# State-space groups as a pipeline, with u and the outputs regrouped through DRAM

## The chip, the cores and the metric

The kernel runs on one core of a Trainium2 chip. The time is device microseconds of one launch. It is written with a tile framework: a scheduler fixes the order of the instructions on each engine when the kernel is built, and each engine then runs its own list in that order. TensorE does the matmuls, VectorE and ScalarE the elementwise work, GpSimd (called POOL in the profile) and SP mostly issue DMAs.

## What is computed

A decoder trunk of two layers over x of 512 positions and 1024 channels, all float32. In each layer one projection of the normalised x gives ten groups of 512 columns, four mixers work on them, and a second projection takes their gated results back to x:

```
for layer in range(DEPTH):                       # DEPTH = 2
    h = rms_norm(x, norm_g[layer])
    a_u, a_g, qd, kd, vd, b_g, c_x, c_g, m_q, m_g = split(h @ w_in[layer], 10)
    y_a = s5_mixer(a_u, ...)        # state space, below
    y_b = differential attention;  y_c = conv + RG-LRU;  y_m = attention to 256 memory tokens
    mixed = concat([y_a*silu(a_g), y_b*silu(b_g), y_c*silu(c_g), y_m*silu(m_g)])
    x = x + mixed @ w_out[layer]
return rms_norm(x, final_norm_g)
```

The state-space mixer has 32 groups of 16 channels, each with 64 complex states. With abar the diagonal of a group and bb its scaled input matrix:

```
x[t] = abar * x[t-1] + bb @ u[t]                 # complex, 64 states a group
y[t] = Re(C x[t]) + d * u[t]
ga, gb = split(gelu(y) @ w_glu);  y_a = ga * sigmoid(gb)
```

## The kernel before

**Projections.** Weights come in pieces of 512 KB (`raw`, two buffers). ScalarE rounds a piece to `whi` (L166), VectorE makes the rest `wlo` (L172), three buffers each, and a projection is three products: hi by hi, lo by hi, hi by lo, with 512 columns moving. In `cm_block` (matmuls L512) the weights are stationary and the result has channels on partitions; in `tm_block` (L532) h is stationary and the result has positions on partitions. The projection of u (`au`) uses `tm_block` with a strided view of h, `h_au`, that takes every fourth position, because the state space works on chunks of T = 4 positions, NC = 128 chunks.

**State space.** `s5` (L920 to L1057) is a generator. Each `yield` hands the turn back to the projections, and a number n in it asks for n ticks; a tick is twelve projection matmuls. First TensorE turns au to U (channel and step on partitions, chunk in the free dimension, 16 blocks), 32 transposes at L927. Then four groups f of four blocks follow one after the other, in each:

- the weights of the chunk's inputs on VectorE, turned by TensorE at L952 (the w-turn) and copied to WT; a small matmul with them (`ms`, L959) plus the direct term gives kq (VectorE), and eight DMAs from GpSimd's queue (L970) spread kq over MT, the matrix of the outputs inside a chunk;
- the states at chunk ends (L990, into `sc`), turned by the phase tables tcq and tsq to xr, scanned over the chunks at L1019 (eight scans), and turned back to xp, the state before each chunk;
- VV, the output weights of the states (VectorE);
- the outputs: U as stationary operand by MT (L1034), xp by VV (L1036), copied to yg at L1038.

After the last group 32 transposes (L1048) bring yg back to channels on partitions, the GELU follows (L1050), and yhi and ylo for the glu projection (matmuls L1215). `mpT`, `qm`, `bg` and others in the rows belong to the other mixers, which run beside it in the same way.

**Norm scale and end.** For layer 0 the norm's scale is broadcast to all 128 partitions by one DMA from ScalarE's queue (L246, `gnb`, 512 KB), and h is x times 1/rms times the scale in one VectorE instruction per half (L295). At the end each of four blocks of x is normalised and leaves in two stores of 256 KB, both from SP's queue (L1296 and L1297).

Of the kernel before, what the change touches and what calls it, by code (L numbers as in the profile page):

```python
# [17 lines left out]
P = 128  # L18
# [36 lines left out]
D_S5 = (1, 1, 1, 2, 2)  # L55
# [35 lines left out]
def tile_kernel(ctx: ExitStack, tc: tile.TileContext, A, out):  # L91
# [7 lines left out]
    sm2 = ctx.enter_context(tc.tile_pool(name="sm2", bufs=9))  # L99
# [96 lines left out]
    gnb = b4([P, D], "gnb")  # L196
# [20 lines left out]
    for l in range(DEPTH):  # L217
        for n in ORDER[l]:
# [14 lines left out]
            elif n in ("q", "k", "v", "au"):  # L233
# [166 lines left out]
    f2_re = const.tile([P, 32], F32, tag="f2_re", name="f2_re")  # L400
    f2_im = const.tile([P, 32], F32, tag="f2_im", name="f2_im")
# [89 lines left out]
    VV = [const.tile([P, 4, 2, T, 16], F32, tag=f"VV{i}", name=f"VV{i}") for i in range(2)]  # L491
    MT = const.tile([P, 2, T, 4, 16], F32, tag="MT", name="MT")
# [69 lines left out]

    def h_au():
        hi = [a.rearrange("p k (c s) -> p k s c", s=T) for a in cur["hi"]]
        lo = [a.rearrange("p k (c s) -> p k s c", s=T) for a in cur["lo"]]
        return ((lambda k, t: hi[k // 4][:, k % 4, t, :]), (lambda k, t: lo[k // 4][:, k % 4, t, :]))
# [279 lines left out]

    bbx = const.tile([P, 32, 16], F32, tag="bbx", name="bbx")
# [8 lines left out]
    def s5_params(l, R):  # L856
        while "par" in st.live:
            yield
        B, Cw = R["B"], R["Cw"]

# [54 lines left out]
    def au_evac(au):  # L915
        def f(s, a):
            S.copy(au[:, :, :, T - 1 - s, :].rearrange("p q g h -> p (q g) h"), a.rearrange("p (a h) -> p a h", h=16))
        return f

    def s5(l, R):  # L920
        au = R["au"]
# [8 lines left out]
        yg = b8([P, T, 16, 2, 16], "yg")  # L930
# [3 lines left out]
        for f in range(4):  # L934
            qs = slice(4 * f, 4 * f + 4)
# [12 lines left out]
            wd = t1.rearrange("p (q g) d h -> p q (g d h)", g=2)  # L948
# [380 lines left out]
```

## Time and profile before

| | |
|---|---|
| median of three runs | 917.92 us (917.91 to 918.27) |
| the profiled execution | 918.38 us, span 916.6 us |
| TensorE busy | 888.9 us, 97% |
| VectorE busy | 658.6 us, 72% |
| ScalarE busy | 510.6 us, 56% |
| GpSimd busy | 43.0 us, 5% |
| DMA | 90.59 MB, 99 GB/s mean |
| granted clock of TensorE | 0.999 of full speed |

The span is the profiled stretch of one execution; 1.8 us of the measured time lie outside it. A busy share is a mean over stages that differ: the span begins with 8.5 us without a matmul, and in the state-space rounds (215 to 338 us in layer 0, 650 to 800 us in layer 1) VectorE is far busier than its mean. A row of the profile names the line of the kernel, the engine and the operation, then what it writes and reads by the program's names without numbers (`xr<-u,u`). Bracketed text behind a row of a timeline is the time the engine sat idle before it and what ended that; a row without it followed at once.

### The profile page before, as it was taken

The numbers are of one execution on the slowest core, as the hardware profiler recorded it, in microseconds if no ns is written. First come the engines' busy times: TensorE is split into PE (matmuls) and PEld (weight loads), VectorE is DVE, ScalarE is ACT, GpSimd is POOL, SyncE is SP. The second block draws the span as 40 slices with busy tenths as digits, with TensorE's granted clock in tenths as the row PEclk, the third lists the DMA queues.
The fourth block names the chain that finished last, engine by engine and source line by source line (L and its number), as shares of the span: only waits on it lengthen the run. The fifth ranks groups of instructions, "written<-read, shape, count | busy, mean of one in ns | idle before, by whom it ended". The sixth has DMA issues, their size and how long they took to land.

```text
span 916.6 us, 12496 instructions
## 1 busy us (share of the span) xinstructions
PE 888.9 (97%) x4538; PEld 747.8 (82%) x4538; DVE 658.6 (72%) x1314; ACT 510.6 (56%) x1031; POOL 43.0 (5%) x94
## 2 busy tenths in 40 slices
PE   5999999999999999999999999999999999999997
PEld 4788888987888788888888888898878888788885
DVE  5984888678999946883374677764889988667343
ACT  6684787985433355821554578766645453854133
POOL 1001000001110100000100000000101110000000
PEclk9999999999999999999999999999999999999999
DMA  6733432212132226433343332432121313152322
GB/s 200 203 114 103 140 92 69 64 53 73 50 93 73 73 93 185 142 107 108 115 149 93 92 92 69 139 92 69 50 70 50 96 31 98 60 184 93 103 81 93
DMA packets 81072, 90.59 MB, mean 99 GB/s; under 512 B 23793, under 2 KB 58226, under 8 KB 81010
## 3 DMA queue, kind: packets, MB, share of 16 engines
q1 hardware_dynamic: 77986, 85.98, 30.1%
q10 hardware_dynamic: 720, 2.62, 0.8%
q0 software_dynamic: 2304, 1.18, 0.6%
q8 instruction: 36, 0.59, 0.3%
q14 instruction: 26, 0.21, 0.1%
HBM read 84.92 MB, written 4.19 MB: 97 GB/s over the span
## 4 chain that ended last, share of the span: by engine, by line
PE 69%; DVE 22%; ACT 6%; issue 2%; DMA 1%; DVEq 0%; SPq 0%; ACTq 0%
PE acc L532 38%; PE acc L512 12%; DVE u L340 5%; PE acc L1215 5%; DVE wlo L172 3%; DVE xr L1019 2%; PE tp L1036 2%; PE ms L677 1%; PE tp L305 1%; PE tp L830 1%; DVE VV L340 1%; PE sc L642 1%; DVE wt L340 1%; PE sc L643 1%; ACT whi L166 1%
## 5 line engine op out<-in xcount | busy, mean ns | idle before, releaser
L166 ACT CAST whi<-raw 128x1024 fp32r<-128x1024 f32 x136 | 143.2, 1053 | 227.9 <-PE acc L532 117.6
L172 DVE TENSOR_TENSOR wlo<-raw,whi 128x1024 fp32r<-128x1024 f32 x136 | 166.2, 1222 | 121.5 <-ACT whi L166 117.8
L512 PE MATMUL acc<-hThi,whi 128*128 128x512 f32 x384 | 153.8, 400 | 0.0
L512 PE MATMUL acc<-hThi,wlo 128*128 128x512 f32 x384 | 152.1, 396 | 0.0
L512 PE MATMUL acc<-hTlo,whi 128*128 128x512 f32 x384 | 152.0, 396 | 0.0
L532 PE MATMUL acc<-whi,hThi 128*128 128x512 f32 x256 | 104.1, 407 | 0.8 <-ACT whi L166 0.8
L532 PE MATMUL acc<-wlo,hThi 128*128 128x512 f32 x256 | 101.4, 396 | 0.0
L532 PE MATMUL acc<-whi,hTlo 128*128 128x512 f32 x256 | 101.0, 395 | 0.0
L532 PE MATMUL acc<-wlo,mxh 128*128 128x512 f32 x256 | 100.1, 391 | 0.0
L532 PE MATMUL acc<-whi,mxh 128*128 128x512 f32 x256 | 100.1, 391 | 0.0
L532 PE MATMUL acc<-whi,mxl 128*128 128x512 f32 x256 | 100.1, 391 | 0.0
L512 PEld LDWEIGHTS acc<-hThi,wlo 128*128 128x128 f32 x384 | 72.2, 188 | 14.5
L512 PEld LDWEIGHTS acc<-hThi,whi 128*128 128x128 f32 x384 | 72.3, 188 | 13.2
L512 PEld LDWEIGHTS acc<-hTlo,whi 128*128 128x128 f32 x384 | 72.4, 188 | 13.1
L532 PEld LDWEIGHTS acc<-whi,hThi 128*128 128x128 f32 x256 | 56.2, 220 | 9.0 <-ACT whi L166 1.2
L532 PEld LDWEIGHTS acc<-whi,hTlo 128*128 128x128 f32 x256 | 56.3, 220 | 7.8 <-DVE hTlo L308 0.2
L532 PEld LDWEIGHTS acc<-wlo,hThi 128*128 128x128 f32 x256 | 56.6, 221 | 7.2
L532 PEld LDWEIGHTS acc<-whi,mxl 128*128 128x128 f32 x256 | 48.1, 188 | 9.8
L532 PEld LDWEIGHTS acc<-wlo,mxh 128*128 128x128 f32 x256 | 48.1, 188 | 9.7
L532 PEld LDWEIGHTS acc<-whi,mxh 128*128 128x128 f32 x256 | 48.1, 188 | 9.7
L970 POOL DMA_DIRECT2D MT<-kq x64 | 32.1, 509 | 364.2 <-DVE kq L340 363.9
L653 ACT ACTIVATE e<-sc,nmx 128x128 f32<-128x128 f32 (+3 forms) x64 | 33.1, 524 | 6.6 <-DVE nmx L649 5.4
(310 smaller groups left out, 1643.8 us busy)
## 6 DMA issues: line engine op xcount, KB each, us to landing
raw<-in_w_in_dram SPq DMA_DIRECT2D x80, 512.0 KB, 3.7
raw<-in_w_out_dram SPq DMA_DIRECT2D x32, 512.0 KB, 3.3
raw<-in_w_mem_kv_dram SPq DMA_DIRECT2D x16, 512.0 KB, 3.4
x<-in_x_dram SPq DMA_DIRECT2D x8, 512.0 KB, 5.2
raw<-in_s_w_glu_dram SPq DMA_DIRECT2D x16, 256.0 KB, 2.9
mt<-in_mem_dram SPq DMA_DIRECT2D x4, 512.0 KB
xd<-x SPq DMA_DIRECT2D x4, 512.0 KB, 4.2
x<-xd SPq DMA_DIRECT2D x4, 512.0 KB, 5.5
```

What stands on the lines that cost most here:

```text
L166: S.copy(hi, wbuf[j])
L172: V.tensor_tensor(out=lo, in0=raw, in1=hi, op=ALU.subtract)
L305: lastins["pe"] = PE.transpose(pt[:, k, :], h[:, kk * 128:(kk + 1) * 128], ident)
L340: V.tensor_tensor(out=o, in0=a, in1=b, op=op)
L512: PE.matmul(a[j][:, :ncol], w[:, kk, c], h(k), start=(hf == 0 and i == 0), stop=(hf == 1 and i == 3 * nh - 1))
L532: PE.matmul(a[t], h(k, t), w[:, kk, :], start=(p == 0 and kk == 0 and i == 0), stop=(p == np_ - 1 and kk == 1 and i == 2))
L642: PE.matmul(s[:, m, :M], qh[:, m, h, :], kT[m][:, h, :M], start=True, stop=False)
L653: S.activation(e[:, m, :N], s[:, m, :N], AF.Exp, bias=nmx[:, m:m + 1], scale=0.125, accum_out=sm[:, m:m + 1])
L970: G.dma_start(out=MT[g * 64 + 64 - n:g * 64 + 64, g, t], in_=kq[g * 64:g * 64 + n])
L1019: V.tensor_tensor_scan(out=xr_[i][:, j, :], data0=dec, data1=xr_[i][:, j, :], initial=0.0, op0=ALU.mult, op1=ALU.add)
L1036: PE.matmul(y[:, j, :], xp[i][:, j, :], VV[i][:, j].rearrange("p g t h -> p (g t h)"), start=False, stop=(i == 1))
L1215: PE.matmul(a, w[:, k, s, j * 128:(j + 1) * 128], h[:, 2 * hf + k, :], start=(hf == 0 and i == 0), stop=(hf == 1 and i == 5))
```

## The change

- **Start.** Only one row of the norm's scale is loaded (4 KB), and TensorE spreads it over the partitions by two matmuls with a row of ones, into PSUM (`sc`); h reads it from there in layer 0.
- **au.** It is made by `cm_block`, weights stationary, h moving, so channels are on partitions. Each of its four blocks is stored to DRAM (`aud`) by GpSimd's queue, and eight DMAs of 128 KB read it back as U. The 32 transposes of L927 are gone.
- **Outputs.** MT and VV are now the stationary operands and U and xp the moving ones (both were laid out anew for it, so MT's eight DMAs move pieces of 64 bytes instead of 256). The result has outputs on partitions and chunks in the free dimension. It is copied to `ys`, stored to DRAM (`yd`) by four DMAs and read back as `yl` by one, all in GpSimd's queue. The GELU reads yl. The 32 transposes of L1048 are gone.
- **Pipeline.** The outputs of group f-1 are issued after the states of group f; the weights of the next group are begun before the turn back. The GELU of group f-1 comes four ticks after its outputs, the last one after a further tick behind the others.
- **Smaller.** kq has one buffer (it had two), the pool `sm2` ten instead of nine, the conv works on 509 to 512 columns without a padded copy, and the last store of the kernel leaves from ScalarE's queue.

The core of the diff:

```diff
-    gnb = b4([P, D], "gnb")
+    grow = b4([1, D], "grow")
+    one = b2([1, P], "one")
+    V.memset(one, 1.0)
...
-    S.dma_start(out=gnb, in_=A["norm_g"][0, :].partition_broadcast(P))
+    S.dma_start(out=grow, in_=A["norm_g"][0:1, :])
...
+    gnp = sc2((P, 2, 512))
+    for half in range(2):
+        PE.matmul(gnp[:, half], one, grow[:, 512 * half:512 * half + 512], start=True, stop=True)
+    gnb = gnp.rearrange("p a b -> p (a b)")
...
-    def au_evac(au):
-        def f(s, a):
-            S.copy(au[:, :, :, T - 1 - s, :].rearrange("p q g h -> p (q g) h"), a.rearrange("p (a h) -> p a h", h=16))
+    def au_evac(R, u):
+        def f(j, a):
+            c = 2 * u + j
+            ac = R["au"][:, c]
+            S.copy(ac, a.rearrange("p (c r) -> p r c", r=T))
+            G.dma_start(out=R["aud"][c * P:(c + 1) * P], in_=ac)
         return f
...
-        for f in range(4):
-            pt = tp()
-            for j in range(4):
-                q = 4 * f + j
-                PE.transpose(pt[:, j, :], au[:, q].rearrange("p g r h -> p (g r h)"), ident)
-            S.copy(U[:, 4 * f:4 * f + 4, :], pt)
-            yield
+        src = R["aud"].rearrange("(q g h) s c -> g s h q c", q=16, g=2)
+        for g in range(2):
+            for r in range(T):
+                k = g * 64 + r * 16
+                G.dma_start(out=U[k:k + 16], in_=src[g, T - 1 - r])
+        yield D_U
...
-            kq = tiny.tile([P, 4, 16], F32, tag="kq", name=nm("kq"))
+            kq = tiny.tile([P, 4, 16], F32, tag="kq", bufs=1, name=nm("kq"))
...
-                    G.dma_start(out=MT[g * 64 + 64 - n:g * 64 + 64, g, t], in_=kq[g * 64:g * 64 + n])
+                    G.dma_start(out=MT[g * 64 + 64 - n:g * 64 + 64, :, t, g], in_=kq[g * 64:g * 64 + n])
...
+        def outputs(f):
+            y = tp()
+            for j in range(4):
+                PE.matmul(y[:, j, :], MT[:, j].rearrange("p t g h -> p (t g h)"), U[:, 4 * f + j, :], start=True, stop=False)
+                for i in range(2):
+                    PE.matmul(y[:, j, :], VV[i][:, j].rearrange("p t g h -> p (t g h)"), xp[i][:, j, :],
+                              start=False, stop=(i == 1))
+            ys = b2([P, 4, NC], "ys")
+            S.copy(ys, y)
+            yd = s5dram.tile([4, 32, T, NC], F32, tag="yd", name=nm("yd"))
+            for t in range(T):
+                G.dma_start(out=yd[:, :, t].rearrange("j k c -> k j c"), in_=ys[32 * t:32 * t + 32])
+            yl = b2([P, T, NC], "yl")
+            G.dma_start(out=yl, in_=yd.rearrange("j k t c -> (j k) t c"))
+            return yl
...
+        for f in range(4):
+            B = states(f)
+            if f:
+                yl = outputs(f - 1)
+            kernel_rows(kq)
+            x_ = turned(f, B)
+            yield D_S5[2]
+            scans(f, x_[0])
+            if f < 3:
+                wd = w_rows(f + 1)
+                turned_back(*x_)
+                yield D_S5[3]
+                c_weights(f)
+            else:
+                c_weights(f)
+                turned_back(*x_)
+                yield D_S5[3]
+            if f:
+                gelu(f - 1, yl)
+            yield D_S5[4]
+            if f < 3:
+                kq = w_turn(f + 1, wd)
+                yield D_S5[5]
+        yl = outputs(3)
...
-            R["au"] = b8([P, 16, 2, T, 16], "au")
-            run(tm_block(h_au(), au_evac(R["au"]), ids))
+            if u == 0:
+                R["au"] = b8([P, 4, T, NC], "au")
+                R["aud"] = s5dram.tile([GW, T, NC], F32, tag="aud", name=nm("aud"))
+            run(cm_block(h_cm(), 8, au_evac(R, u), ids))
...
-                        nc.sync.dma_start(out=ot[:, 0:512], in_=x_[0])
+                        (S if t == NT - 1 else nc.sync).dma_start(out=ot[:, 0:512], in_=x_[0])
```

What the change moves stands in the lists of the engines. On TensorE in layer 0, before, the outputs of the first group (`tp<-VV,xp` and `tp<-MT,U`) are strewn between projection matmuls:

```order
L512 MATMUL acc<-hThi,wlo 128x512
L512 MATMUL acc<-hThi,whi 128x512
L1036 MATMUL tp<-VV,xp_468 128x128
L1034 MATMUL tp<-MT,U 128x128
L1036 MATMUL tp<-VV,xp_467 128x128
L1036 MATMUL tp<-VV,xp_468 128x128
L1034 MATMUL tp<-MT,U 128x128
```

Now they follow the states of the second group (`sc<-U,WT`) as one block, with MT and VV stationary:

```order
L1003 MATMUL sc<-U,WT 128x128
L1003 MATMUL sc<-U,WT 128x128
L1003 MATMUL sc<-U,WT 128x128
L1010 MATMUL tp<-U,MT 128x128
L1012 MATMUL tp<-xp_467,VV 128x128
L1012 MATMUL tp<-xp_468,VV 128x128
L1010 MATMUL tp<-U,MT 128x128
L1012 MATMUL tp<-xp_467,VV 128x128
```

The block stands right behind the last three of the eight state matmuls; the projection matmuls that stood between the outputs stand elsewhere.

On VectorE in layer 1, second group, before, around the product that begins the next group's kq (`kq<-pv,cst`); `u<-sc,tcq` is the first use of the group's states:

```order
L340 TENSOR_TENSOR VV<-wt_1271,wt_1272 64x4x64 x2
L340 TENSOR_TENSOR u_1274<-tab,tab 128x512
L340 TENSOR_TENSOR u_1275<-tab,tab 128x512
L340 TENSOR_TENSOR tsq<-u_1274,u_1275 128x512
L340 TENSOR_TENSOR u_1274<-sc,tcq 128x512
L340 TENSOR_TENSOR u_1275<-sc,tsq 128x512
L172 TENSOR_TENSOR wlo<-raw,whi 128x1024
L340 TENSOR_TENSOR xr_1278<-u_1274,u_1275 128x512
L340 TENSOR_TENSOR kq<-pv,cst 128x64
L340 TENSOR_TENSOR u_1274<-sc,tcq 128x512
```

Now, the same place (`xr<-sc,tcq` is the first use of the states):

```order
L348 TENSOR_TENSOR tcq<-tcq,u 128x512
L173 TENSOR_TENSOR wlo<-raw,whi 128x1024
L348 TENSOR_TENSOR u<-tab,tab 128x512
L348 TENSOR_TENSOR xr_1275<-sc,tcq 128x512
L348 TENSOR_TENSOR tsq<-tsq,u 128x512
L348 TENSOR_TENSOR kq<-pv,cst 128x64
L348 TENSOR_TENSOR u<-sc,tsq 128x512
L348 TENSOR_TENSOR xr_1276<-sc,tcq 128x512
L348 TENSOR_TENSOR xr_1275<-xr_1275,u 128x512
L716 SCALAR_TENSOR_TENSOR bg<-th,acc 128x512
```

The product stands two instructions behind the first use of the states; it had three more (and a wlo) between them before. VV's instructions have moved ahead, out of these rows.

In GpSimd's queue in layer 1, before, the MT stores of the second and third group:

```order
L970 DMA MT<-kq 16x64 x2
L970 DMA MT<-kq 32x64 x2
L970 DMA MT<-kq 48x64 x2
L970 DMA MT<-kq 64x64 x2
L970 DMA MT<-kq 16x64 x2
L970 DMA MT<-kq 32x64 x2
L970 DMA MT<-kq 48x64 x2
L970 DMA MT<-kq 64x64 x2
```

Now, the MT stores of the second group and the first two of the third, with the outputs' stores yd and the load yl among them:

```order
L981 DMA MT<-kq 16x4x16 x2
L981 DMA MT<-kq 32x4x16
L1018 DMA yd<-ys 32x4x128 x4
L981 DMA MT<-kq 32x4x16
L981 DMA MT<-kq 48x4x16 x2
L981 DMA MT<-kq 64x4x16
L1020 DMA yl<-yd 128x512
L981 DMA MT<-kq 64x4x16
L981 DMA MT<-kq 16x4x16 x2
```

Four stores and one load stand inside what were eight MT stores in a row, and the last MT store of a group is behind the load.

## Rows read from the trace of the kernel before

**Rows 1.** The page, part 1: busy us (share of the span) and instructions.

```profile
PE 888.9 (97%) x4538; PEld 747.8 (82%) x4538; DVE 658.6 (72%) x1314; ACT 510.6 (56%) x1031; POOL 43.0 (5%) x94
```

**Rows 2.** Waits of TensorE: us in total, times, longest.

```profile
PE tp L305 <- DVE h L295: 8.5, 1, 8.5
PE tp L1036 <- DVE xp L340: 4.6, 7, 1.0
...
PE tp L1048 <- ACT yf L1050: 0.3, 1, 0.3
```

**Rows 3.** A window: its us, busy us of PE, PEld, DVE, ACT, POOL.

```profile
243.00:271.00 28.00, 27.37 (x155) 23.33 (x154) 27.36 (x50) 9.01 (x15) 4.00 (x8) 1.00 0.23 71
```

**Rows 4.** Timeline of TensorE at au's transposes: start us, us, instruction.

```profile
203.28 0.66 PE L927 MATMUL tp<-cst,au 128*128 128x128 f32 x4 [0.24 <-ACT pT L669]
203.70 0.48 PE L512 MATMUL acc<-hThi,wlo 128*128 128x512 f32 x1
204.01 0.60 PE L927 MATMUL tp<-cst,au 128*128 128x128 f32 x4
204.37 0.48 PE L512 MATMUL acc<-hThi,whi 128*128 128x512 f32 x1
```

**Rows 5.** The chain of waits in order of time: start us, us, what.

```profile
0.74 5.22 DMA x<-in_x_dram
...
386.45 48.99 PE acc L532 x216
```

**Rows 6.** Timeline of TensorE in au's projection, layer 1.

```profile
604.22 0.40 PE L532 MATMUL acc<-whi,hThi 128*128 128x512 f32 x1
...
605.39 0.39 PE L532 MATMUL acc<-whi,hTlo 128*128 128x512 f32 x1
```

**Rows 7.** Line L1086, GpSimd: duration ns min/median/max, first and last start.

```profile
L1086 POOL DMA_DIRECT2D bd<-in_lru_w_x_dram x4: 622/628/640, 89.5 to 442.5; - x4
```

**Rows 8.** Line L970, the MT stores: duration ns, and us to landing.

```profile
L970 POOL DMA_DIRECT2D MT<-kq x64: 488/507/527, 214.8 to 749.5; - x64
...
DMA to landing us min/median/max: 1.5/2.4/5.2
```

**Rows 9.** Timeline of the start, VectorE and TensorE.

```profile
7.69 1.42 DVE L295 SCALAR_TENSOR_TENSOR h<-x,rstd,gnb 128x512 f32<-128x512 f32 x2
...
14.59 0.63 PE L532 MATMUL acc<-whi,hTlo 128*128 128x512 f32 x1
...
15.02 0.63 PE L532 MATMUL acc<-whi,hThi 128*128 128x512 f32 x1
```

**Rows 10.** Timeline of the end, queue of SP.

```profile
912.95 0.33 SPq L1297 DMA_DIRECT2D out_dram<-x  x1
913.38 0.38 SPq L1296 DMA_DIRECT2D out_dram<-x  x1
```

**Rows 11.** Timeline of VectorE, layer 1, second group, from xr.

```profile
699.86 0.69 DVE L340 TENSOR_TENSOR xr<-u,u 128x512 f32<-128x512 f32 x1
700.46 0.22 DVE L340 TENSOR_TENSOR kq<-pv,cst 128x64 f32<-128x64 f32 x1
...
703.31 2.32 DVE L1019 TENSOR_TENSOR_SCAN xr<-mag,xr 128x128 f32<-128x128 f32 x7
```

**Rows 12.** Timeline of TensorE at the states, layer 0.

```profile
217.09 1.95 PE L990 MATMUL sc<-U,WT 128*128 128x128 f32 x16
218.79 0.47 PE L512 MATMUL acc<-hThi,whi 128*128 128x512 f32 x1
```

**Rows 13.** Lines L1038 and L1050, ScalarE: duration ns min/median/max.

```profile
L1038 ACT COPY yg<-tp x8: 584/586/589, 241.7 to 785.3; 128x512 f32<-128x512 f32 x8
...
L1050 ACT ACTIVATE yf<-tp x8: 1067/1092/1127, 318.4 to 794.4; 128x512 f32<-128x512 f32 x8
...
L1050 ACT ACT_TABLE_LOAD  x1: 1283/1283/1283, 785.9 to 785.9; - x1
```

**Rows 14.** The page, part 5: busy us, mean ns of one, idle before.

```profile
L166 ACT CAST whi<-raw 128x1024 fp32r<-128x1024 f32 x136 | 143.2, 1053 | 227.9 <-PE acc L532 117.6
```

More of the change, by code (lines that the diff above doesn't have):

```diff
@@ L845, in s5_load @@
         R["B"], R["Cw"] = B, Cw
+    s5dram = ctx.enter_context(tc.tile_pool(name="s5dram", bufs=2, space=bass.MemoryType.DRAM))
     bbx = const.tile([P, 32, 16], F32, tag="bbx", name="bbx")
@@ L952, in s5 @@
                 PE.transpose(pt[:, j, :], wd[:, j], ident)
+            pk = ms((P, 4, 2, 16))
+            for j in range(4):
+                PE.matmul(pk[:, j].rearrange("p g h -> p (g h)"), wd[:, j],
+                          cs_[:, 8 * f + 2 * j:8 * f + 2 * j + 2, :].rearrange("p g h -> p (g h)"), start=True, stop=True)
             for i in range(2):
@@ L985, in s5, with states @@
             c_i = bc(cc_[:, 1, qs], 2, sh)
-            yield D_S5[1]
+            for dst, x1, x2, op in ((VV[0], a_r, a_i, ALU.add), (VV[1], a_i, a_r, ALU.subtract)):
+                tt(t1, x1, c_r, ALU.mult)
+                tt(t2, x2, c_i, ALU.mult)
+                for g in range(2):
+                    hs = slice(g * 64, (g + 1) * 64)
+                    tt(dst[hs, :, :, g], t1[hs], t2[hs], op)
+        def states(f):
             B = sc2((P, 2, 4, NC))
@@ L1029, in s5 @@
-            tt(v2, xm[1], tcm, ALU.mult)
-            V.scalar_tensor_tensor(out=xp[1][:, :, 1:], in0=v1, scalar=-1.0, in1=v2, op0=ALU.mult, op1=ALU.subtract)
-            yield D_S5[3]
-            y = tp()
-            for j in range(4):
-                PE.matmul(y[:, j, :], U[:, 4 * f + j, :], MT[:, :, :, j, :], start=True, stop=False)
-                for i in range(2):
-                    PE.matmul(y[:, j, :], xp[i][:, j, :], VV[i][:, j].rearrange("p g t h -> p (g t h)"),
-                              start=False, stop=(i == 1))
@@ L1038, in s5 @@
-            S.copy(yg[:, :, qs].rearrange("p t q g h -> p t (q g) h"),
-                   y.rearrange("p q (g t h) -> p t (q g) h", g=2, t=T))
+            xo = [a[:, :, 1:] for a in xp]
+            tt(xo[0], xm[0], tcm, ALU.mult)
+            tt(v, xm[1], tsm, ALU.mult)
+            tt(xo[0], xo[0], v, ALU.subtract)
+            tt(xo[1], xm[0], tsm, ALU.mult)
+            tt(v, xm[1], tcm, ALU.mult)
+            V.scalar_tensor_tensor(out=xo[1], in0=xo[1], scalar=-1.0, in1=v, op0=ALU.mult, op1=ALU.subtract)
@@ L1040, in s5 @@
             yield D_S5[4]
+            if f < 3:
+                kq = w_turn(f + 1, wd)
+                yield D_S5[5]
+        yl = outputs(3)
         yhi = b8([P, 4, L], "yhi", F32R)
         ylo = b8([P, 4, L], "ylo", F32R)
-        ygf = yg.rearrange("p t q g h -> p t (q g h)")
-        for c in range(4):
-            pt = tp()
-            for t in range(T):
-                PE.transpose(pt[:, t, :], ygf[:, t, c * 128:(c + 1) * 128], ident)
-            yf = b2([P, NC, T], "yf")
-            S.activation(yf.rearrange("p c t -> p t c"), pt, AF.Gelu_apprx_tanh)
-            yff = yf.rearrange("p c t -> p (c t)")
-            S.copy(yhi[:, c, :], yff)
-            tt(ylo[:, c, :], yff, yhi[:, c, :], ALU.subtract)
-            if c == 3:
-                S.activation(ti(1, "sq0"), yff[:, 0:1], AF.Exp)
+        for f in range(4):
+            if f == 3:
+                yield
+                gelu(3, yl)
+            yff = yf[:, f].rearrange("p c t -> p (c t)")
+            S.copy(yhi[:, f, :], yff)
+            tt(ylo[:, f, :], yff, yhi[:, f, :], ALU.subtract)
```

107 lines of the change are left out of this document (52 added, 55 removed).

## The prediction

> **What bounds the kernel now.** I read the page's busy shares first: TensorE is busy 888.9 of 916.6 us [rows 1], so almost every microsecond of matmul that goes should shorten the run, and the 27.7 us that are left say what else could. The waits of TensorE came next [rows 2]: 8.5 us before the first transpose, 4.6 us in seven waits of the output matmuls for xp, and three waits of 0.3 us for the GELU's yf (one is shown). Then the windows of the state-space rounds, of which one is shown [rows 3]: there VectorE is busy 27.36 of 28 us, so in these stretches it sets the pace as much as TensorE. The profiled execution took 918.38 us, 1.8 us of it outside the span; the median of the runs shown is 917.92, 0.46 us less.
>
> **Transposes (gone: 32 of au, 32 of yg, in 16 groups of four).** Two groups took 0.42 and 0.36 us from start to next start, mean 0.39, and the 512-column matmul behind each is followed after 0.31 us instead of 0.227 (216 matmuls in 48.99 us) [rows 4, 5], 0.08 more. 16 x 0.47 = 7.5 us, all of it TensorE time in its order: **-7.5**. The swapped state-space matmuls have the same count and size; they are costed at nothing.
>
> **au with weights stationary.** Five of au's matmuls step in 1.17 us, 0.234 each [rows 6], against 0.227. 2 x 96 x 0.0075 = **-1.4**. Its evacuation stays a copy of 128x512.
>
> **Round trip of U.** After the last au copy (0.6): one aud store (issue 0.63, as bd's, whose 256 pieces are as many as a U load's [rows 7]; landing bounded by MT's 1.5 and 5.2 [rows 8], taken 3 for its 256 KB), eight U loads (8 x 0.63 = 5.0; landing 2.4 as MT's median): 11.6 us, at worst 0.6 + 0.6 + 5.2 + 5.0 + 5.2 = 16.6. In the order of TensorE 31 us of matmuls (some 130 at 0.227) stand between the end of au and the first states, in layer 0, and 32 in layer 1. Hidden: 0.
>
> **Start.** x lands 5.22 us after its start at 0.74 [rows 5], beside a broadcast of the norm scale of as many bytes; then squares, root and reciprocal, and the first h at 7.69 [rows 9]. The chain of waits starts there. Without the broadcast x can land earlier by what 512 KB take; x itself took 5.2 us for as much while sharing, so the gain is between 0 and 2.6. The two new K=1 matmuls sit before h, but their row of 4 KB should land near 0.74 + 2.4 = 3.1, and at the 0.43 us which 512 columns took there [rows 9], times four as a bound for f32, they end near 6.6, one microsecond below 7.69. Taken: **-1.2**.
>
> **End.** The two last stores leave SP one behind the other at 912.95 and 913.38 [rows 10]; on two queues the second goes with the first: **-0.4**.
>
> **The waits for xp: what goes and what comes.** Outputs of a group now stand after the next group's states, so the xp waits of 4.6 us could all go. But VectorE's work is the same, and it gets a new kind of wait. kq has one buffer instead of two: the product that starts the next kq must wait until all eight MT stores of the last have landed, and in POOL's queue the last MT store stands behind four yd stores and the yl load, which wait for the outputs. The order puts that product early: in layer 1, second group, two VectorE instructions behind the first use of the states. In before the same product ran with no idle before it [rows 11]. Its chain from the end of the states: 12 output matmuls (a run of eight states took 1.70 us [rows 12], so 2.6), copy 0.6 [rows 13], four yd issues 2.5 and four MT issues 2.0 (0.63 and 0.51 [rows 7, 8]), yl 0.6, the last MT 0.5, its landing 2.4: 11.2 us. VectorE is there after two steps of 0.6 [rows 11]: it **stands still for 10 us**. TensorE does not yet feel it: 26.7 us of matmuls (the order's rows at 0.227, transposes at 0.11) stand between those states and the next w-turn, and VectorE owes it 9.2 us of steps (11 x 0.6 and eight scans at 0.33), ready at 1.2 + 10 + 9.2 = 20.4, 6.3 early. In the third group the slack goes: by the same counting, with 0 at 5 us before the first states, outputs(1) end at 65.6, its chain of 8.6 behind them at 74.5 with two semaphores, and VectorE, late by then, reaches its product at 70.7, is held 3.8 us and has 16.5 us of work to the last VV: 91.0, where TensorE wants it at 89.5. Outputs(2) wait 1.5. In layer 0 the product falls early only for the fourth group: VectorE, released at 52.7 us after the first states by a transposed tile of TensorE, has 47 us of work to xp(3), which TensorE wants 45.6 us later (98.3); with 0.6 to 1.5 of hold that is 2 to 3 us, taken 2.5. Together 4.0 against 4.6: **-0.6**. At landings of 1.5 it would be about 1.5 (-3.1), at 5.2 in both stages of the chain about 20 (+15).
>
> A rule speaks against this part. In the rows, MT stores issued while VectorE was 98% busy took 488 to 527 ns each [rows 3, 8]. The Trainium skill's "SBUF — State Buffer" (the box on the "DVE blocks DMA" trap, section "SBUF: two separate sides") says that a DMA issued by GpSimd starves for descriptors while VectorE holds the port pair they share, and gives 620 ns growing to 3100. By that rule each of the ten issues in the chain would cost up to 2.5 us more and the rounds would lose tens of microseconds; the trace does not bear it out for the subtractions and products that fill VectorE here.
>
> **GELU behind the DRAM round trip.** After outputs(3): copy 0.6, four yd issues 2.5, landing 2.4, yl 0.6 and landing 2.4, GELU 1.1 [rows 13], then on ScalarE a cast 1.05 [rows 14] and a table load 1.3 [rows 13] that the order puts ahead of yhi 0.6: 12.5 us. In layer 1 TensorE has 14.7 us of matmuls between outputs(3) and the first that needs it, in layer 0 about 16. Hidden with 2 us to spare; the three waits of 0.3 for yf go, and I put as much back for a late yl: **0**. Without cover each microsecond more costs one.
>
> **Sum.** -7.5 - 1.4 - 1.2 - 0.4 - 0.6 = -11.1: 918.38 becomes 907.3 in a profiled run, 906.8 by the median. **Forecast 907.**
>
> **Rivals.**
> - *No hold.* If MT and yd land in 1.5 us, the xp waits cost 1.5 instead of 4.0 and yf's 0.9 go for good: 907 - 3.4 = 903.5, and with the whole 2.6 at the start 902. For it: the shortest landings in the trace. Against: their median, and 64-byte pieces, four times as many in each MT store.
> - *VectorE decides the rounds.* The holds take away slack, and every wlo and qm behind them comes late too. With waits of 9 us in place of 4: 912. For it: the window that is 98% busy.
> - *The queue of POOL makes it slower.* One mechanism: yd, yl and MT in one in-order queue. With x us more per landing, the two landings in a chain cost layer 0 2x and layer 1 4x at the xp waits, and each layer's GELU 2x less its slack of about 2.5. The 11.1 us are gone at x = 1.7 (10.2 + 1.8), that is at landings of 4.1 instead of 2.4; at the 5.2 which the trace has as its longest, x = 2.8 gives 16.8 + 6.2 = 23, 930. For it: 5.2 occurs, aud and yd go to DRAM, and the stores have more pieces. Against: the median of 64 stores. Issues that grow instead of landings would do the same, ten to a chain; 527 ns as the longest of 64 leaves that 1 in 50, counted here.
> - *Two queues and the small row do nothing.* The start is held by DMA latency and the new matmuls: 1.6 less, 908.5.
>
> On piece sizes the trace shows only landings, not causes: the Trainium skill's "DMA: Bandwidth & Descriptors" (Specifications) asks for at least 512 bytes per piece and says smaller ones are read, modified and written. MT's go from 256 to 64 bytes, U and yd have 512. By that rule only MT is slowed; no run here shows by how much, and it would push toward the slower rivals.
>
> **Chances.** Forecast with the start rival (904.5 to 910): 0.52. No hold: 0.18. VectorE decides (910 to 916): 0.16. POOL's queue (over 916): 0.14, of which a third ends within 0.2% of before (1.8 us, about what a measurement of this kernel can tell from no change). Below 900 there is nothing left to gain: 7.5 + 1.4 + 2.6 + 0.4 + 4.6 + 0.9 = 17.4. Range 900 to 916, the upper end into the slower rival's neighbourhood. Faster 0.84, same 0.06, slower 0.10.
>
> **What would show it.** TensorE's busy time lower by 8 to 9 us and no rows of transposes of au and yg; the first h near 6.5; idle of VectorE before a kq product, released by a DMA of MT: some 10 us in layer 1, second group, 4 in the third, about 1 in layer 0; waits of the output matmuls of group 2 in layer 1 and group 3 in layer 0 for xp. Wrong if kq products show no idle (then the rounds gain), if the states wait for U, or if the glu matmuls wait for ylo over 1 us.

## The result: 925.3 us, slower than before, and the profile after

| | before | after |
|---|---|---|
| median | 918.1 us (917.9 to 918.4) | 925.3 us (925.1 to 925.9) |
| ratio, 95% interval | | 1.0079 (1.0063 to 1.0095) |
| span of the profiled execution | 916.6 us | 923.5 us |
| granted clock of TensorE, mean | 0.999 | 0.991 |

The forecast was 907 us, its range 900 to 916. The page of after, part 1 (busy us, share of the span, instructions), answers to [rows 1]:

```profile
PE 888.0 (96%) x4478; PEld 736.8 (80%) x4478; DVE 657.8 (71%) x1315; ACT 512.6 (56%) x1028; POOL 81.3 (9%) x150
```

The transposes are gone (60 matmul instructions fewer in the count), yet TensorE is busy as long as before, in part because some of its matmuls ran at half clock. Its waits, us in total, times, longest, against [rows 2]:

```profile
PE acc L518 <- DVE ag L716: 5.9, 2, 4.0
PE tp L1012 <- DVE xp L348: 5.0, 1, 5.0
PE sc L258 <- DMA grow<-in_norm_g_dram: 3.2, 1, 3.2
PE tp L960 <- DVE wt L348: 2.2, 3, 0.9
```

Seven short waits for xp (4.6 us) have become one of 5.0, and a new row stands above it: projections wait for VectorE to empty their accumulators (`acc`). The windows of the rounds show where (12 us each; busy us of PE, PEld, DVE, ACT, POOL; granted clock, DMA share, GB/s). Before had VectorE at 11.3 to 12 of 12 in the stretches from 240 to 312, as in [rows 3]; two of its windows, then those of after:

```profile
300.00:312.00 12.00, 12.00 (x64) 10.20 (x63) 11.88 (x26) 2.65 (x4) 4.02 (x8) 1.00 0.31 95
312.00:324.00 12.00, 10.96 (x65) 8.96 (x64) 10.17 (x18) 5.97 (x9) 0.00 (x0) 1.00 0.27 83
```

```profile
240.00:252.00 12.00, 12.00 (x63) 10.17 (x62) 8.27 (x12) 1.64 (x2) 7.25 (x13) 1.00 0.54 148
300.00:312.00 12.00, 12.00 (x65) 10.34 (x64) 8.02 (x14) 2.26 (x3) 6.45 (x12) 1.00 0.43 127
312.00:324.00 12.00, 6.95 (x36) 5.40 (x35) 11.96 (x28) 3.75 (x5) 0.77 (x2) 0.98 0.31 99
324.00:336.00 12.00, 8.82 (x35) 7.87 (x36) 9.48 (x19) 3.07 (x6) 1.62 (x3) 0.59 0.16 49
768.00:780.00 12.00, 8.82 (x45) 7.21 (x43) 11.88 (x27) 4.66 (x6) 0.00 (x0) 1.00 0.17 60
```

In after VectorE first stands still for some 4 of 12 us while TensorE is full; then VectorE is full and TensorE stands still; then the clock is low. The low clock is seen in the timeline of TensorE behind the wait for xp (start us, us, instruction; in brackets the idle time before it and what ended it):

```profile
325.30 0.80 PE L1012 MATMUL tp<-xp,VV 128*128 128x128 f32 x2 [5.04 <-DVE xp L348]
327.97 0.79 PE L518 MATMUL acc<-hThi,whi 128*128 128x512 f32 x1 [1.88 <-DVE ag L716]
328.56 0.63 PE L518 MATMUL acc<-hTlo,whi 128*128 128x512 f32 x1
...
333.98 0.39 PE L518 MATMUL acc<-hTlo,whi 128*128 128x512 f32 x1
334.21 0.39 PE L518 MATMUL acc<-hThi,wlo 128*128 128x512 f32 x1
```

A matmul of 512 columns steps by 0.43 us behind the wait (328.56 to the next at 328.99) and by 0.23 again from 333.98. Read from such windows and markers, layer 0 loses about 8.2 us of idle TensorE and 3.8 of slow clock (the matmuls from 325.30 to 333.98 took 6.8 us, and at the full rate of the rows around them they would take 3.0), layer 1 7.0 and 1.6: 21 us. With the 7 us by which after is slower, that leaves a gain of some 14 in the rest. (Before is not free of idle there: 4.9 us of TensorE in the windows from 240 to 348 and 684 to 792.)

The start and the end, against [rows 9, 10] (VectorE's first h; the last norm product and the last store):

```profile
6.97 1.41 DVE L303 SCALAR_TENSOR_TENSOR h<-x,rstd,sc 128x512 f32<-128x512 f32 x2 [0.92 <-PE sc L258]
...
918.87 0.75 DVE L1351 SCALAR_TENSOR_TENSOR x<-x,rstd,gnb 128x512 f32<-128x512 f32 x1
919.62 0.38 ACTq L1354 DMA_DIRECT2D out_dram<-x  x1
```

The first h is 0.72 us earlier, not 1.2: x lands earlier, but h then waits 0.92 for the spreading matmuls. From the last norm product to the end of the span it takes 4.6 us, before 4.4: the second queue gained nothing.

### The profile page after: what moved, and what is told of

Same layout as the page of the kernel before. It is cut to its first block, busy times and chain, and to the rows that moved or that the text cites. A ratio compares the mean times of both kernels' runs of the same rounds, so it can differ in the third digit from the quotient of the medians.

```text
span 923.5 us, 12446 instructions
## 1 busy us (share of the span) xinstructions
PE 888.0 (96%) x4478; PEld 736.8 (80%) x4478; DVE 657.8 (71%) x1315; ACT 512.6 (56%) x1028; POOL 81.3 (9%) x150
## 4 chain that ended last, share of the span: by engine, by line
PE 48%; DVE 9%; ACT 3%; issue 1%; DMA 1%; POOL 0%; DVEq 0%; POOLq 0%; ACTq 0%
PE acc L538 26%; PE acc L518 9%; PE acc L1272 4%; DVE u L348 1%; DVE xr L1057 1%; PE tp L831 1%; DVE wlo L173 1%; DVE wt L348 1%; DVE xr L348 1%; PE ms L678 1%; PE tp L1012 1%; PE tp L824 1%; PE sc L806 1%; PE tp L313 1%; DVE xp L348 1%
## 5 line engine op out<-in xcount | busy, mean ns | idle before, releaser
L173 DVE TENSOR_TENSOR wlo<-raw,whi 128x1024 fp32r<-128x1024 f32 x136 | 165.7, 1222 | 145.7 <-ACT whi L167 142.0
L518 PE MATMUL acc<-hThi,whi 128*128 128x512 f32 x448 | 179.9, 402 | 5.9 <-DVE ag L716 5.9
L518 PE MATMUL acc<-hThi,wlo 128*128 128x512 f32 x448 | 176.8, 395 | 0.1
L518 PE MATMUL acc<-hTlo,whi 128*128 128x512 f32 x448 | 176.7, 394 | 0.0
L538 PE MATMUL acc<-whi,hThi 128*128 128x512 f32 x192 | 77.2, 402 | 0.8 <-ACT whi L167 0.8
L538 PE MATMUL acc<-wlo,hThi 128*128 128x512 f32 x192 | 75.7, 394 | 0.0
L538 PE MATMUL acc<-whi,hTlo 128*128 128x512 f32 x192 | 75.7, 396 | 0.0
L538 PEld LDWEIGHTS acc<-whi,hThi 128*128 128x128 f32 x192 | 36.4, 190 | 8.7 <-ACT whi L167 1.2
L538 PEld LDWEIGHTS acc<-whi,hTlo 128*128 128x128 f32 x192 | 36.5, 190 | 7.8 <-DVE hTlo L316 0.2
L538 PEld LDWEIGHTS acc<-wlo,hThi 128*128 128x128 f32 x192 | 36.6, 190 | 7.1
L648 DVE TENSOR_REDUCE mx<-sc 128x2 f32<-128x256 f32 (+3 forms) x32 | 26.3, 822 | 14.6 <-PE sc L646 14.3
```

The source lines that it names most:

```text
L173: V.tensor_tensor(out=lo, in0=raw, in1=hi, op=ALU.subtract)
L518: PE.matmul(a[j][:, :ncol], w[:, kk, c], h(k), start=(hf == 0 and i == 0), stop=(hf == 1 and i == 3 * nh - 1))
L538: PE.matmul(a[t], h(k, t), w[:, kk, :], start=(p == 0 and kk == 0 and i == 0), stop=(p == np_ - 1 and kk == 1 and i == 2))
L648: V.tensor_reduce(out=mx, in_=s[:, :, :N], op=ALU.max, axis=AX.X)
```

## The experiments

Four theories stood at first. *Theory 1*: the pipeline's order; VectorE has the last group's state too late for TensorE. *Theory 2* (the GELU rival below): ScalarE, held in its order by the GELU's wait for the DRAM round trip, delays the casts of the weights. *Theory 3*, the prediction's: kq's one buffer holds VectorE. *Theory 4*: late weight loads. *Theory 5* came later, from the runs.

**One part of the change alone.** e1 is the kernel before with `au` in `cm_block` and U through DRAM; e2 has the start of the change as well. Its expectation names the end too, but the kernel that ran has both last stores in SP's queue.

> The kernel before with one part of the change: the au projection computed channel-major, written to DRAM by eight stores of two chunks' worth, and U loaded back with eight DMAs (the 32 transposes and the token-major au are gone); the states rounds, outputs, GELU, start and end are those of before. By the markers of the two traces the au part gained about 0.8 us and U's transposes about 3.1 us, and nothing of it was given back in the rounds. Theory 1 (the loss lies in the pipelined rounds: VectorE's list brings the last group's state late): 914 us, a ratio of 0.994 to 0.998. Rival (the round trip through DRAM itself is what costs: U's loads on POOL's queue hold the kernel rows and the other transfers behind them): not faster, 918 us or more.

Measured: 912.76 us (ratio 0.9942, 0.9927 to 0.9957).

> The same as the run before it, and the start (norm scale row spread by TensorE) and the end (last store on ScalarE's queue) of the change as well. The trace of after has its first layer's markers 0.5 to 0.7 us early from the start alone, and its end 0.2 us later than it should be. Theory 1: 913.5 us, 0.3 to 0.8 us under the run before it, which three rounds may not tell apart. Rival (the start does nothing, as its time is given back by the first waits): equal to the run before it within 0.2 us.

Measured: 912.15 us (0.9936, 0.9921 to 0.9950). With au in `cm_block` and without the transposes of U the kernel gains 5.3 us, so U's round trip costs nothing that shows; the loss is in the rounds. The start's 0.6 is inside the intervals.

**kq and the GELU.** e3 gives kq two buffers:

```diff
-            kq = tiny.tile([P, 4, 16], F32, tag="kq", bufs=1, name=nm("kq"))
+            kq = tiny.tile([P, 4, 16], F32, tag="kq", name=nm("kq"))
```

> The changed kernel with two buffers for kq in place of one, so that the next group's kernel rows are made without waiting for the eight stores of the last one. The prediction priced this hold at up to 10 us of VectorE. Theory of the prediction (the kq hold paces VectorE): 2 to 4 us faster than the changed kernel, 921 to 923 us. Theory 1 and the GELU rival: no change, 925 us within 1 us, as the trace of after shows a single wait of 0.7 us there.

Measured: 924.99 us (1.0083, 1.0062 to 1.0103): no change. Theory 3 falls. In after's trace the whole hold is this row of VectorE's waits:

```profile
DVE kq L348 <- DMA MT<-kq: 0.7, 1, 0.7
```

e4 moves `if f: gelu(f - 1, yl)` behind the next w-turn and its yield.

> The changed kernel with the GELU of group f-1 moved in the program behind the next group's turn of the weights and its waits, so that ScalarE comes to it two to four ticks later and finds the rows back from DRAM. ScalarE waited 13.2 us in 6 GELUs for them (the largest 4.5 and 3.0). Rival theory (ScalarE held by the round trip delays the weight casts, these VectorE, this TensorE): the wait falls under 4 us in sum, TensorE's idle time in the two state stages falls by 4 us or more, 921 us or less. Theory 1 (VectorE's list sets the last group's chain): the wait falls just so, and the time stays within 1.5 us of 925.

Measured: 925.08 us (1.0072, 1.0055 to 1.0089). ScalarE's wait for the load fell only from 13.2 to 9.5 us, so this alone is a weak test of Theory 2; e15 below, which has 14.0 us of the same waits and is fast, refutes it.

**Where VectorE's work stands.** e5 changes the yields: `yield D_S5[3]` becomes `yield 1` in groups 0 to 2 and `yield 5` in group 3.

> The changed kernel with one wait between two matmul blocks fewer in each of the first three rounds, and five instead of two behind the last group's turning back, so that TensorE has more other matmuls in its list between the last group's states and its outputs: in layer 0 the outputs of group 3 begin 44 matmuls of the big projections behind the states (53 before) but end 18 further ones apart, in layer 1 132 behind (98 before); the states themselves come 26 and 33 matmuls earlier. Theory 1 (TensorE comes to the last outputs before VectorE has made the state, and its clock falls after the wait): layer 1's waits go (about 7 us idle and 1.6 us of slow clock), layer 0's shrink or stay, 917 to 921 us. Rival (the DRAM round trips or the weight casts are late whatever the order): 924 to 926 us.

Measured: 935.73 us (1.0188, 1.0171 to 1.0205), 10 us worse, with 12.4 us in two waits of projections for `ag` in place of 5.9. Both expectations missed: moving the waits in the program only moved the stalls. e6 leaves out `c_weights(3)`.

> The changed kernel without the last group's output weights: group 3 uses those of group 2 (this part of the output is left out), so that some 2.8 us of VectorE between its scans and its turning back fall away in each layer. Theory 1: TensorE's 5.0 us wait for xp in layer 0 falls to about 2, the one in layer 1 by the same, and the slow clock behind them shrinks: 918 to 922 us. Rival (VectorE only waits there for a weight cast, so that its own work is covered): 924 to 926 us.

Measured: 915.86 us (0.9973, 0.9964 to 0.9982): 5.7 us of VectorE work fewer, 9.4 us of time. VectorE does pace TensorE there. e7 fills the wait:

```diff
+        fill = tp()
+        for n in range(20):
+            PE.matmul(fill[:, n % 4, :], WT[0][:, n % 4].rearrange("p g c -> p (g c)"), U[:, 12 + n % 4, :], start=True, stop=True)
         yl = outputs(3)
```

> The changed kernel with 20 matmuls 128x128 more in each layer ahead of the last group's outputs, their result never read: 4.6 us of TensorE at 0.23 us each, put where TensorE waits 5.0 us for xp in layer 0. If the granted clock fell because TensorE stood still there, the 8 us stretch at half clock behind it goes in layer 0 (4.4 us less), and the added matmuls cost nothing there; in layer 1 the wait lies at another matmul and they cost up to 4.6 us: 921 to 926 us in sum, with layer 0's stretch at a granted clock over 0.9 in place of 0.59. Rival (the clock falls there for another reason, as the load of all engines): the stretch keeps its clock and the time grows by up to 9 us, 926 to 934 us.

Measured: 927.06 us (1.0092, 1.0075 to 1.0109). TensorE in e7 waits 2.2 us there, not 6.9, and the window that had 0.59 keeps its clock:

```profile
324.00:336.00 12.00, 10.29 (x55) 8.91 (x56) 9.70 (x15) 5.30 (x10) 2.74 (x5) 1.00 0.34 110
```

So in layer 0 the clock fell because TensorE had stood still. The total did not gain: the profiled run is 5.0 us ahead of after at the last states of layer 1 (751.4 against 756.4) and 0.6 ahead at the last outputs, in front of which the other 20 matmuls stand.

**Order or outputs?** e8 puts the groups one after the other with the waits of before, and keeps the new outputs. e9 keeps the pipeline and takes back the old outputs (U and xp stationary, 16 transposes a layer, GELU from PSUM).

> The changed kernel with the groups one after the other as before the change (weights, turn, kernel rows, states, output weights, turning, scans, turning back, outputs, and the waits 1, 1, 1, 2, 2 of before between them) in place of the pipeline; U and the outputs go through DRAM, with swapped operands, and the start and the end are the change's. Theory 1 (only the pipeline's order loses): the gain of U and au stays, that of the output transposes (about 3.7 us by the prediction) comes to it: 907 to 911 us. Rival (the outputs' round trip costs, through ScalarE's wait or the transfers): 914 us or more.

Measured: 940.52 us (1.0242, 1.0221 to 1.0263).

> The changed kernel with the outputs of before: the state matrices as stationary operands again, token-major copies, 16 transposes and GELU from PSUM, and no round trip of the outputs through DRAM; the pipeline's order and its waits stay as the change has them. With the run that had the U part and the start of the change but the old order and the old outputs (912.15 us), the changed kernel (925.3) and the one with the old order and the new outputs (940.5) it fills a square of two. Theory 1 as it was first put (the pipeline's order loses): 921 us or more. Rival, after the last runs (the new outputs, with their round trip in ScalarE's and the queues' lists, lose, and the pipeline's order takes part of that back): 908 to 914 us.

Measured: 908.13 us (0.9892, 0.9877 to 0.9907). Theory 1 falls as it was put: the pipeline's order gains 4.0 us with the old outputs (912.15 to 908.13; e9 also has the change's end and its smaller items, which e2 lacks) and 15 with the new (940.5 to 925.3). The new outputs lose 17 and 28. e8 was no clean test of the order alone: one of its largest stalls (5.1 us, at 343.7) is in gate accumulators that wait behind the memory attention.

**Two that missed.** e10 cuts VectorE's work of a round into pieces with a yield after each; e11 sets `NRAW` to 3 and the pool `sm2` to 8.

> The changed kernel with VectorE's state work of a round cut into more pieces over the same number of matmul blocks: tables, a block, the products with the states, a block, the scans and the next rows, a block, the turning back, a block, the output weights (in the last group scans, turning back, a block, output weights). Theory 1 in its narrower form (VectorE is idle for weight remainders in one stretch and has 10 us of state work in a piece in the next, so that TensorE outruns it): VectorE's 8.3 of 12 us in the stretches 240 to 252, 276 to 288 and 300 to 312 fill up, TensorE's waits of 5 and 4 us shrink, 915 to 921 us. Rival (the sum of VectorE's work between the last states and the last outputs decides, wherever it stands): 924 to 928 us.

Measured: 923.77 us (1.0075, 1.0052 to 1.0099). VectorE stayed at 7.85 of 12 us in 240 to 252: the pieces did not fill the gap.

> The changed kernel with three buffers instead of two for the raw weights, paid for with two small tiles fewer in the pool (8 in place of 10), so that a weight load is issued one chunk earlier. In the trace of after ScalarE waits 3.1 us for a raw load ahead of VectorE's idle 3.9 us at 305 to 309, between the last group's states and its outputs. Rival theory 4 (late weight loads set the waits): TensorE's waits in the state stages fall by 4 us or more and the time to 919 us or less. Theory 1: the casts come earlier but wait for their own buffers, 923 to 927 us; the smaller pool could cost more.

Measured: 929.04 us (1.0128, 1.0111 to 1.0145). Two things changed at once, so this does not refute Theory 4 by itself; e15, which is fast with two raw buffers, does.

**What holds the outputs' rows.** In the engines' lists of after, as they were built, the rounds are unequal: 66, 93 and 105 projection matmuls from one group's first states to the next in layer 0, 67, 100 and 96 in layer 1. In e9 they are 66, 84, 84 and 67, 84, 84, from the same yields. So something in the new outputs changes the order that is built. The first differing row of VectorE's list, after against e15 below (layer 0, in the turning of group 1):

```
- L173 TENSOR_TENSOR wlo_2703<-raw_2557,whi_2701 128x1024
  L348 TENSOR_TENSOR u_2622<-tab_313,tab_314 128x512
  L348 TENSOR_TENSOR xr_520_2631<-sc_2583,tcq_2623 128x512
```

A weight remainder, `wlo`, stands ahead of the state's products; in e15 it comes 25 rows later, behind the scans. e12 takes yl out of the pool of small tiles:

```diff
+        ylb = b8([P, 4, T, NC], "ylb")
-            yl = b2([P, T, NC], "yl")
+            yl = ylb[:, f]
```

> The changed kernel with one difference: the four yl (the outputs as they come back from DRAM) are quarters of one large tile instead of four tiles from the pool of ten small tiles, from which VectorE's tables, products, states and the rows of the weights come too. Theory 5 (the change's loss is the pool: ys and yl hold small tiles through the stores' and the load's landings until the GELU, so the state work of the next round waits for a tile and stands later in the engines' lists): in the order the first states of the four groups stand 66, 84, 84 matmuls of the projections apart in layer 0 instead of 66, 93, 105, and 67, 84, 89 instead of 67, 100, 96 in layer 1, as in the run with the old outputs (908.13 us); the time falls to 903 to 909 us, with VectorE over 11 of 12 us busy at 240 to 252, 276 to 288 and 300 to 312. Rival (the round trip through DRAM itself, its 20 DMAs a layer on GpSimd's queue, or ScalarE's GELU waiting for them): 918 us or more, VectorE at 8 of 12 as in after.

Measured: 921.25 us (1.0039, 1.0026 to 1.0053): between the two. Layer 0 did as Theory 5 says, layer 1 did not. The windows of e12, and TensorE's timeline in layer 1:

```profile
240.00:252.00 12.00, 12.00 (x64) 10.16 (x63) 11.90 (x21) 2.73 (x4) 7.26 (x13) 1.00 0.49 139
756.00:768.00 12.00, 5.85 (x24) 5.27 (x24) 2.50 (x7) 7.28 (x24) 0.00 (x0) 0.50 0.15 48
```
```profile
758.60 2.93 PE L806 MATMUL sc<-kv,qm 128*128 128x256 f32 x12 [9.82 <-ACT me L814]
765.08 2.93 PE L806 MATMUL sc<-kv,qm 128*128 128x256 f32 x12 [3.55 <-ACT me L814]
```

Three heads of the memory attention follow each other in the list with next to nothing between, and each waits for the softmax of the one before; the first of these sat behind the last group's state in VectorE's list. e13 takes the round trip away:

```diff
-            yd = s5dram.tile([4, 32, T, NC], F32, tag="yd", name=nm("yd"))
...
-            return yl
+            return ys
```

> The changed kernel without the outputs' round trip: neither the stores to yd nor the loads of yl, the GELU reads ys in its place (the regrouping of the outputs is left out). Theory 5: as the run with yl in a large tile, 902 to 909 us, and the difference between the two is what the round trip costs beside the pool, which I put at 0 to 3 us. Rival (the transfers or GpSimd's queue are the cost): this run alone is fast, 15 us or more below the one with yl in a large tile.

Measured: 902.42 us (0.9836, 0.9822 to 0.9849). With e12 alone that would have spoken for the rival, the round trip itself. e14 keeps the round trip and takes no tile for it:

```diff
-        yf = b8([P, 4, NC, T], "yf")
+        yf = b8([P, 4, T, NC], "yf")
-            yl = b2([P, T, NC], "yl")
+            yl = yf[:, f]
-            S.activation(yf[:, f].rearrange("p c t -> p t c"), yl, AF.Gelu_apprx_tanh)
+            S.activation(yl, yl, AF.Gelu_apprx_tanh)
```

> The changed kernel with the whole round trip of the outputs, but no tile of its own for what comes back: the load lands in yf, the GELU works in place there, and the reordering of steps and chunks is done by the rounding to yhi and the subtraction of ylo. Every tile pool is as free as without the round trip, and the order on TensorE is that of the run without it, the memory heads of layer 1 72 matmuls of the projections apart (in the run with yl in a large tile two of them stood 7 apart, and the third behind them, since that tile was the last of its pool). Theory 5, widened to both pools (what costs is not the round trip but the tile that it holds, from whichever pool): 902 to 908 us, no wait of TensorE over 1.5 us in the two state stages. Rival (the round trip itself: the transfers, GpSimd's queue, ScalarE's waits for the load): 915 us or more.

Measured: 903.16 us (0.9843, 0.9829 to 0.9857). The medians of e13 and e14 differ by 0.7 us, which is inside the intervals: no cost of the round trip is seen. ScalarE still waits for it, in GELUs that nobody waits for (its waits, e14):

```profile
ACT yf L1024 <- DMA yf<-yd: 12.2, 5, 3.5
```

**One word.** e15 is the changed kernel with yl from the pool of four tiles of 4 KB:

```diff
-            yl = b2([P, T, NC], "yl")
+            yl = b4([P, T, NC], "yl")
```

> The changed kernel with one word changed: yl comes from the pool of four tiles of 4 KB in place of the pool of ten tiles of 2 KB. The round trip, the GELU's place and layout and all waits in the program are those of the change. In the order the rounds are again 66, 84 and 84 matmuls of the projections long in layer 0, and the memory heads of layer 1 stand 72 apart but for the last (68). Theory 5: 903 to 908 us. Rival (the in-place GELU or its rounding was what helped in the last run): 918 us or more.

Measured: **902.56 us** (0.9829, 0.9815 to 0.9842), 15.4 us under before and 22.7 under the change. The page's first line, TensorE's longest waits and the windows of e15:

```profile
PE 880.8 (98%) x4478; PEld 732.4 (81%) x4478; DVE 658.4 (73%) x1315; ACT 510.0 (57%) x1026; POOL 81.4 (9%) x150
```
```profile
PE sc L258 <- DMA grow<-in_norm_g_dram: 2.4, 1, 2.4
PE tp L668 <- DVE e L660: 1.4, 2, 0.7
PE tp L960 <- DVE wt L348: 1.3, 2, 0.8
```
```profile
240.00:252.00 12.00, 12.00 (x64) 10.17 (x63) 11.90 (x21) 2.72 (x4) 7.27 (x13) 1.00 0.49 139
300.00:312.00 12.00, 11.40 (x53) 9.20 (x52) 11.91 (x30) 4.35 (x6) 3.00 (x6) 1.00 0.19 53
312.00:324.00 12.00, 12.00 (x65) 10.16 (x64) 9.45 (x13) 4.17 (x6) 2.19 (x4) 1.00 0.51 153
324.00:336.00 12.00, 12.00 (x59) 10.13 (x58) 5.66 (x8) 5.98 (x8) 0.56 (x1) 1.00 0.33 107
744.00:756.00 12.00, 12.00 (x60) 10.18 (x59) 11.91 (x26) 4.71 (x6) 0.00 (x0) 1.00 0.23 63
```

VectorE is busy 10.5 to 12 of 12 us from 240 to 312, and TensorE has 11.40 to 12 of 12 in the stages where after had 6.95, 8.82 and 8.82. (e15 reaches the last states of layer 0 at 290.8 us and those of layer 1 at 734.2, after at 297.3 and 756.4, so its window 744 to 756 answers to after's 768 to 780.) The same place in VectorE's timeline, first after, then e15:

```profile
243.48 0.69 DVE L348 TENSOR_TENSOR tcq<-tcq,u 128x512 f32<-128x512 f32 x1
247.87 1.22 DVE L173 TENSOR_TENSOR wlo<-raw,whi 128x1024 fp32r<-128x1024 f32 x1 [3.70 <-ACT whi L167]
249.02 0.68 DVE L348 TENSOR_TENSOR u<-tab,tab 128x512 f32<-128x512 f32 x1
```
```profile
243.57 0.69 DVE L348 TENSOR_TENSOR tcq<-tcq,u 128x512 f32<-128x512 f32 x1
244.29 0.69 DVE L348 TENSOR_TENSOR u<-tab,tab 128x512 f32<-128x512 f32 x1
245.01 0.69 DVE L348 TENSOR_TENSOR xr<-sc,tcq 128x512 f32<-128x512 f32 x1
```

Until here both lists are the same. In after the remainder waits for ScalarE's cast (247.87), and that for a weight buffer that TensorE still reads:

```profile
246.79 1.05 ACT L167 CAST whi<-raw 128x1024 fp32r<-128x1024 f32 x1 [4.66 <-PE acc L518]
```

Meanwhile the state's products, which need nothing more, stand behind it. In e15 they go first. Here VectorE idles 3.7 us, and it does so in other rounds too. From a layer's first states to its last outputs VectorE is idle, by the traces, 12.6 us in layer 0 and 20.9 in layer 1 of after, 9.4 and 15.1 of it before remainders that wait for a cast; in e15 it is 1.5 and 8.6, with 1.0 and 0.8 before such remainders. The two stretches are 14 and 12 us shorter in e15. That is the mechanism of the loss: VectorE stands still behind an instruction that is not ready, and the time is missing later when TensorE wants the state. The remainder is not the only row that can hold the list. In e10 it held VectorE for 12.4 us instead of 24.5, gates that wait for ScalarE held it for 15.6 (2.3 in after), and the idle sum was as large: 36.0 us against 33.5.

e16 is e13 with one more small tile held from the outputs to the GELU, and no transfer into it; e17 is e14 with the start of before.

> The run without the round trip (GELU from ys, regrouping left out), with one small tile more for each group, touched by GpSimd at the outputs and by ScalarE at the GELU and otherwise idle. Theory 5 in its plain form (any tile held from the outputs to the GELU costs, as it is one of ten): 915 us or more, against 902.4 without it. Theory 5b (it is that the tile is filled by a transfer which starts late and lands late, and the state work that gets the tile next stands behind it): 901 to 905 us; its order in the list, with rounds of 66, 84, 84, speaks for this one.

Measured: 902.56 us (0.9836, 0.9822 to 0.9849): holding a tile of the pool costs nothing, and by e14 and e15 the load into another tile costs nothing either. What costs is the two together, a tile of this pool that the load fills; that the load's lateness matters was not tested by itself.

> The run with the GELU in place (903.16 us), with the start of the kernel before: the norm scale broadcast by one DMA of 512 KB, no spreading by TensorE. By the markers of the traces the new start is worth 0.7 us, by the two earlier runs with and without it 0.6: 903.8 us, 0.2 to 1.2 us above. The prediction's figure was 1.2. Rival (the start does nothing): 903.2 within 0.3.

Measured: 903.09 us (0.9840, 0.9827 to 0.9854), against 903.16: no gain of the start is seen. The intervals are 1.2 us to either side, so a gain of the 0.6 would not show.

## Why the prediction was wrong

**Transposes and au (-7.5, -1.4): right.** e1 gained 5.3 where these terms give 3.75 + 1.4 = 5.2. Old against new outputs (e9, e15) is 5.6 where they give 3.75, or 4.65 with the 0.9 of the yf waits, which the prediction gave back. Once the stalls are gone TensorE's busy time is lower by 8.1 us, as forecast (8 to 9).

**Round trip of U (0): right.** In after the 16 loads landed in 3.6 to 6.8 us with 5.2 as the median, twice what was taken; in e1, with 3.3 to 8.3, no states waited for them.

**The waits for xp (-0.6): this step failed**, twice. The hold of kq was priced at 10 and 3.8 us and is 0.7 in all. MT's stores land in 2.8 us (taken: 2.4), in e15 in 2.2, so neither the landings nor the pieces of 64 bytes were the miss. The place named for the 10 us, layer 1, second group, reads so in after (VectorE's timeline, against [rows 11]; the last row is MT's line):

```profile
699.82 1.23 DVE L173 TENSOR_TENSOR wlo<-raw,whi 128x1024 fp32r<-128x1024 f32 x1 [7.58 <-ACT whi L167]
700.96 0.69 DVE L348 TENSOR_TENSOR u<-tab,tab 128x512 f32<-128x512 f32 x1
...
702.88 0.22 DVE L348 TENSOR_TENSOR kq<-pv,cst 128x64 f32<-128x64 f32 x1
...
DMA to landing us min/median/max: 1.5/2.8/5.2
```

VectorE does stand still there, but four instructions ahead of the product, for a weight remainder; when it comes to the product, kq is free. The list shown ahead of the prediction has this row: `wlo` stands between tcq and the first product with the states, where before it stood behind two such products. And the sentence "VectorE's work is the same" left out where that work stands. It was priced as if each list ran without gaps up to the named wait; the runs showed 33.5 us of idle VectorE in the rounds, and behind it 15 us of idle TensorE and 5.4 of slow clock. I had looked for new waits among those that the change adds to the program; the loss came from a tile's pool, which changes the order that is built, and so from a wait that was there before, wlo for whi (117.8 us in before, 142.0 in after, 113.0 in e15). The pipeline, with the smaller items, gains 4.0 with the old outputs, not 0.6.

**GELU (0): right**, for a reason that the prediction gave: it is hidden (e14, e15).

**Start (-1.2) and end (-0.4): no gain seen.** The first h came 0.7 earlier, and nothing of it shows in the time (e17). The end was tested in no run of its own; by the traces its last stretch grew by 0.2 us. The rival that said so was right as far as the runs can tell.

**The rivals.** "No hold" had the right hold and the wrong sign. "POOL's queue" had the right side, and the wrong mechanism: e15 has the same transfers in the same queue and is fast. (Its sum is slightly off: 10.2 + 1.8 is 12.0, and 11 us are gone at x = 1.6.) "VectorE decides" named the engine, and asked for 9 us of waits; but it made its lateness out of the hold. The test that I set, "wrong if kq products show no idle (then the rounds gain)", came true in its first half only.

**The clock** stood in no term. A stall of 5 to 7 us in one place cost some 3.8 us more at half clock.

**Open.** Why the order comes out differently when a load lands in a tile of that pool was not seen, only that it does: yl in a small tile 925.3, in a tile of 4 KB 902.6, in none 903.2, with the same work and transfers. The same holds for the large tile in layer 1 of e12.

## What to carry to other kernels

Where a change adds a transfer, ask from which pool its tile comes and who takes tiles from there, and try the loaded tile from another pool: here that one word was worth 22.7 us. A tile from the pool of large ones did it in layer 0 alone (e12), so read the order that comes out. Price a change in the order in which the engines' lists are built by comparing the distances between stages in them, not only by the waits that the program adds; an instruction that is not ready (here a weight remainder) and stands ahead of ready ones in the list of an engine that sets the pace can cost the slack of a whole stage. And when TensorE waits some microseconds in one piece, count the slow clock behind it.

## What the runs showed of the hardware

GpSimd's issues do not slow down beside a full VectorE: in e15, from 240 to 252, 13 DMA issues took 7.27 us, 0.56 each, while VectorE was busy 11.90 of 12 us; in after the same 13 took 7.25 us with VectorE busy 8.27. The Trainium skill's "SBUF — State Buffer" (section "SBUF: two separate sides", the "DVE blocks DMA" trap) gives 620 ns growing to 3100 beside a `tensor_copy` of VectorE; in this window, with VectorE's products, subtractions and scans, the issues stay under its lower figure. In e12 the window of 12 us in which a stall of TensorE of 9.8 us ended had a granted clock of 0.50: the lower level, 1.2 GHz, all through it.
